# Four small moves around the change from the embedding product to the gate stage in a hybrid encoder layer: where two frames live, when the lower gate rows load, when the second pair is transposed, and which queue loads h

## The chip, the cores and the metric

The kernel runs on one core of a Trainium2 chip. The metric is device time in microseconds (us) of one execution, as the median of several executions; lower is better. A profile of one further execution is read beside it. TensorE is called PE in the profile, VectorE DVE, ScalarE ACT, GpSimd POOL and SyncE SP.

## What is computed

One layer of a streaming encoder over 2048 prompt rows and 32 decode rows, model width D = 1024, all in float32. Cut to what matters here (`N` is an RMS norm over a row, `rows` are the 2080 rows):

```python
z  = N(h, g_mix) @ w_in                       # six parts of 512 columns
y  = concat(conv_mixer(z), pooling_mixer(z))  # rows x 1024
h  = h + y @ w_out                            # the output projection
e  = p @ w_ple                                # the embedding product, p is rows x 256
h  = h + e * sigmoid(N(h, g_ple) @ w_gate)    # the gate
out = N(h, g_final)
```

The kernel also returns the new convolution and pooling states, which play no part here.

## The kernel before

**Number format.** Products of float32 values are made from halves: each operand is split into a high part (a cast on ACT) and the rest (a subtraction on DVE), and three of the four partial products are formed (`FINE`). The split operands are called frames below when they hold activations, and weight parts when they hold weights.

**Tiles and pairs.** The rows are cut into 17 row tiles: 0 to 15 of 128 rows, and tile 16 with the 32 decode rows. The output projection and the gate go over pairs of row tiles (0 and 1, 2 and 3, and so on; a pair is called by its first tile). One pair is one call of `seven`, a Strassen-Winograd scheme: seven products instead of eight, in the order

```
x 11   y 12   x S2*T2   z S1*T1   z S4*22   x S3*T3   x 22*T4
```

(two or three of them change places for certain pairs). A product is 12 matmuls of 128x128 by 128x512. 11, 12 and 22 are quadrants of a pair's transposed rows, S1 to S4 sums of them, T1 to T4 sums of the weight's quadrants. The results lie in PSUM banks called `x_o`, `y_o`, `z_o` in the output projection, and `x_g`, `y_g`, `z_g` in the gate. `carry` takes an intermediate result out of a bank (`c_o` by DVE, `c_g` by ACT), `out` finishes a quadrant. The dictionary `between`, the last argument of `seven`, holds work that is written down between two products: `step(1)` stands after the first, `step(2)` after the second, `step(3)` after the third, `step(4)` after the fourth. That work prepares the next pair.

**Stages.** After the input projection and the mixers comes the output projection for pairs 0 to 14; the new `h` goes to a buffer in device memory, `h_d` (`done_h`). The embedding product runs in parts (`embed`, L149 on): seven tiles early, and tiles 7 to 14 and 16 in a last part between the output projection and the gate. Its results go to `e_d` in device memory. Each tile of it needs a frame `pps_i`, loaded by `load_pps` (L128) from `pp_d`; the loads are issued up to three tiles ahead. Then comes the gate for pairs 0 to 14; after pair 4 the short tile 16 is worked in (`short_gate`).

**The gate's input.** A pair's upper tile `hn_i` is loaded by rows (`load_rows`, L396), copied by ACT (`ho`, L1530) and transposed by PE in eight transposes into two banks (`pth`, L1532); that is `turned`. The pair's lower tile `hn_{i+1}` is loaded in four quarters by SP (`by_quarters`, L1541) and transposed by DVE's stream transpose in place (`turned_here`, L1547). `prep_g(i)` returns two pieces of work: `first` (loads and the stream transpose) and `second` (PE's transposes, sums on DVE at L1728, splits at L81 and L84), to be done after the second and the third product of the pair before. For pair 2 the loads are issued ahead of that (`ahead`). For pair 0 the two pieces stand behind two of the embedding tiles.

**The gate's weights.** `g_d` in device memory holds the scaled gate weight. Its upper four blocks of rows are `wg_t` (`tops`), its lower four `wg_b` (`bots`, L1386). They are split into the parts 11, T1, T2, T3, 21, 22 and T4 by casts on ACT (L203) and subtractions on DVE (L195, L210); the last subtraction, at L1776, makes T4's source, and after it the lower rows are read for the last time. The embedding weights (`wq`, L1504) lie in a slot that T2 and T4 use later.

**Buffers.** The pools that the change touches: `st` (four slots, tag `t`: carried results, and frames `pps`), `ss` (three slots, tag `s`: the frame sums of L1728 and those of the output projection), `xh` (four slots: `h`, and before it results of the embedding), `ya` (five slots: `hn`, `e`), `cmb` (eight slots: split frames, and `wg_b`). A load into a slot waits until the last reader of what was there before is done.

**What sets the order.** Every engine works in order through its own list, and so does each DMA queue's issuer: SP issues DMAs only, POOL issues DMAs between small computations, ACT some. The order of each list comes from a scheduler that weighs the instructions by its own estimates; the text of the program is one of its inputs, and two constructions tie it: `tc.issue_after(x)` puts what is inside behind `x`, and `keep_in_program_order` keeps single instructions where they are written. So a change of one place can reorder instructions at others. Loads of `h` for the gate are issued by POOL (0.53 us each), those of `hn` and `e` by SP. A finished tile goes out by POOL (L1578), and the last pair's output in four pieces (`normed`, L1643 and L1645).

Of the kernel before, what the change touches and what calls it, by code (L numbers as in the profile page):

```python
# [10 lines left out]
F32R = mybir.dt.float32r  # L11
# [4 lines left out]
P = 128  # L16
# [15 lines left out]
EARLY = 7  # L32
# [4 lines left out]
def trunk(ctx, tc, x_p, x_s, c_conv, c_pool, p_p, p_s, g_mix, w_in, conv_w, conv_b, pool_w,  # L37
          pool_scale, w_out, g_ple, w_gate, w_ple, g_fin, y_p, y_s, sc_p, sp_p, sc_s, sp_s):
    nc = tc.nc
# [6 lines left out]
    h_d = tc.dram_tile([T, D], F32, name="h_d")  # L46
# [33 lines left out]
    def split(hi, lo, src, eng=nc.vector, later=False):  # L80
        ins = nc.scalar.copy(hi, src)  # L81
        if later:
            tc.keep_in_program_order(ins)
        eng.tensor_tensor(lo, src, hi.bitcast(F32), op=ALU.subtract)  # L84
        return ins
# [15 lines left out]
    tiles = [(i * P, P) for i in range(SEQ // P)] + [(SEQ, DEC)]  # L101

    def rows_of(pr, sa, r, n):
        return pr[r:r + n] if r < SEQ else sa
# [22 lines left out]
    def load_pps(t, i, queue, ins=False):  # L127
        n = 4 * tiles[i][1]  # L128
        load = queue.dma_start(t.rearrange("p a k n -> p (a k n)")[:, :n].bitcast(F32), pp_d[i, :, :n])
        return load if ins else t  # L130
# [57 lines left out]
    def weight_source(W, q, k, top, bot, pin=False):  # L188

        b11, b12 = top[:, :NH], top[:, NH:]  # L190
        b21, b22 = (bot[:, :NH], bot[:, NH:]) if bot is not None else (None, None)
        t, x, y = {"11": (b11, None, None), "T1": (b11, b12, b11), "T2": (b11, b22, b11), "T3": (b12, b22, b12),
                   "22": (b22, None, None), "21": (b21, None, None), "T4": (b21, b21, b11)}[q]
        if x is not None:
            ins = nc.vector.tensor_tensor(t, x, y, op=ALU.subtract)  # L195
            if pin:
                tc.keep_in_program_order(ins)
        return t

    def weight_first(W, part, q, pin=False):  # L200

        k, t = part
        ins = nc.scalar.copy(W[q][0][:, k], t)  # L203
        if pin:
            tc.keep_in_program_order(ins)

    def weight_second(W, part, q, pin=False):

        k, t = part
        ins = nc.vector.tensor_tensor(W[q][1][:, k], t, W[q][0][:, k].bitcast(F32), op=ALU.subtract)  # L210
        if pin:
            tc.keep_in_program_order(ins)
        return ins

    def weight_parts(W, tops, bots, *names, order=range(KH), pin=False):

        for q in names:
            at = lambda k: (W, q, k, tops[k], bots[k] if bots else None)
            todo = [(k, weight_source(*at(k), pin)) for k in order[:2]]
            for k in order[2:]:  # L220
                weight_first(W, todo[0], q, pin)
                following = (k, weight_source(*at(k), pin))
                weight_second(W, todo.pop(0), q, pin)
                todo.append(following)
            for part in todo:
                weight_first(W, part, q, pin)
                ins = weight_second(W, part, q, pin)
        return ins
# [130 lines left out]
    def slot(name):  # L359
        return acts[0].tile([P, SLOT], F32R, tag="hn", name=name)  # L360
# [8 lines left out]
    def weight_slot(W, name, *names):  # L369
        t = slot(f"{name}_{names[0]}")  # L370
        c = halves(t)
        W.update({q: c[2 * i:2 * i + 2] for i, q in enumerate(names)})
        return t
# [8 lines left out]
    def ring4(t, name):  # L382
        return t.tile([P, D], F32, tag="t", name=name)
# [9 lines left out]
    def load_rows(pool, name, i, pr, sa=None, queue=nc.sync):  # L393
        r, n = tiles[i]
        t = ring4(pool, f"{name}_{i}")
        queue.dma_start(t[:n], pr[r:r + n] if sa is None else rows_of(pr, sa, r, n))  # L396
        return t

    with ExitStack() as s1:
# [414 lines left out]
        second = second_block()  # L814
# [382 lines left out]
        ahead = {}  # L1197
# [102 lines left out]
    with ExitStack() as s2:  # L1300
        pool = lambda name, bufs: s2.enter_context(tc.tile_pool(name=name, bufs=bufs, reuse_waits="tile"))
        qa, xh, ya, cmb = (pool(*a) for a in (("qa", 2), ("xh", 4), ("ya", 5), ("cmb", 8)))
# [122 lines left out]
        for c in range(EARLY):  # L1425
            if c == EARLY - 2:
# [3 lines left out]
        st, ss = (s2.enter_context(tc.tile_pool(name=name, bufs=bufs, side="right", reuse_waits="tile"))  # L1430
                  for name, bufs in (("st", 4), ("ss", 3)))
# [36 lines left out]
        for i in range(0, NT - 1, 2):  # L1468
# [6 lines left out]
            if last:  # L1475
                n = tiles[NT - 1][1]
# [19 lines left out]
        tops, _ = rows_of_weight(ya, "wg_t", g_d, 0)  # L1496
        weight_slot(W, "wg", *PLACES[0])
        weight_parts(W, tops, None, "11", "T1")
        shared = slot("wq")
        wp = [[shared[:, (2 * k + h) * D:(2 * k + h + 1) * D] for h in range(2)] for k in range(2)]  # L1500
        got = {0: load_pps(st.tile([P, 2, 2, P], F32R, tag="t", name=f"pps_{EARLY}"), EARLY, nc.sync)}
        for k in range(2):
            for h in range(2):
                nc.sync.dma_start(wp[k][h].bitcast(F32), wl_d[k][h])  # L1504
        got[1] = st.tile([P, 2, 2, P], F32R, tag="t", name=f"pps_{EARLY + 1}")
        second_pps = load_pps(got[1], EARLY + 1, nc.sync, True)
        with tc.issue_after(second_pps.ins):
            bots = rows_of_weight(cmb, "wg_b", g_d, 1)[0]
# [13 lines left out]
        def turned(i, t=None):  # L1522
# [9 lines left out]
                    nc.tensor.transpose(pt[:, k * P:k * P + n], o[:n, k], ident[:n, :n])  # L1532
                out.append(pt.rearrange("p (k t) -> p k t", k=KH))
            return out

        def by_quarters(i):

            r, n = tiles[i]
            t = ring4(ya, f"hn_{i}")
            for q in range(4):  # L1540
                nc.sync.dma_start(t[q * 32:q * 32 + 32].rearrange("p (g c) -> p g c", g=4),  # L1541
                                  h_d[r:r + P, q * 256:q * 256 + 256].rearrange("(g p) c -> p g c", p=32))
            return t

        def turned_here(t):

# [51 lines left out]
        def last_pair(i, A, before):  # L1598
# [7 lines left out]
            wp = []  # L1606
            chunk = lambda: wp.extend(load_wp(cmb, "wl", nc.sync))

            h = [load_rows(xh, "h", i + b, h_d, queue=nc.gpsimd) for b in range(2)]
            tt = nc.vector.tensor_tensor  # L1610
            carry, _ = gate_ops(h, [e], P, f"g{i}", i)
            hg = [ring4(ya, f"hg_{b}") for b in range(2)]
# [25 lines left out]
            def normed(b, rf):  # L1638
                r = tiles[i + b][0]
                o, y = hg[b], y_p[r:r + P]  # L1640
                cut = 5 * P
                fixed(nc.vector.tensor_scalar(o[:, :cut], o[:, :cut], scalar1=rf, scalar2=None, op0=ALU.mult))
                nc.sync.dma_start(y[:, :cut], o[:, :cut])  # L1643
                fixed(nc.scalar.activation(o[:, cut:], o[:, cut:], AF.Copy, scale=rf))  # L1644
                (nc.scalar if b else nc.gpsimd).dma_start(y[:, cut:], o[:, cut:])  # L1645

            cols_of = lambda half: slice(half * NH, half * NH + NH)
            at_last = {}
# [68 lines left out]
        def prep_g(i, ahead=False):  # L1717

            A, got = {}, {}
            whole = lambda t: t.rearrange("p k (g t) -> p k g t", g=4)  # L1720

            def put(q, src, view=lambda t: t):
                A[q] = cmb.tile([P, KH, 2, P], F32R, tag="c", name=f"g{i}_{q}")
                split(view(A[q][:, :, 0]), view(A[q][:, :, 1]), src)

            def comb(q, x, y, op, view=lambda t: t):
                t = ss.tile([P, KH, P], F32, tag="s", name=f"g{i}_f{q}")
                nc.vector.tensor_tensor(view(t), x, y, op=op)  # L1728
                return t

            lower = []

            def load():
                got["lower"] = by_quarters(i + 1)
                got["upper"] = load_rows(ya, "hn", i, h_d) if i else first_h

            if ahead:
                load()

            def first():  # L1740
                if not ahead:
                    load()
                lower.extend(turned_here(got["lower"]))

            def second():
                a21, a22 = lower
                s1 = comb("S1", a21, a22, ALU.add, whole)
                a11, a12 = turned(i, got["upper"])
                put("11", a11)
                s2 = comb("S2", s1, a11, ALU.subtract)  # L1750
                s3 = comb("S3", whole(a11), a21, ALU.subtract, whole)
                put("12", a12)
                put("S2", s2)
                s4 = comb("S4", a12, s2, ALU.subtract)
                put("S1", s1)
                put("S3", s3)
                put("S4", s4)
                put("22", a22, whole)

            S[i] = A  # L1760
            return {2: first, 3: second}

        S = {}
        steps = prep_g(0)
        for c in range(len(rest_e)):
            run(c)
            if c in (2, 4):
                steps[2 if c == 2 else 3]()
        W["T2"] = halves(shared)[2:]
        weight_parts(W, tops, bots, "T2")  # L1770
        W["T3"] = halves(seventh("wg_T3"))
# [22 lines left out]
        for i in range(0, NT - 3, 2):  # L1794
            A = S.pop(i)
            following = prep_g(i + 2, not i)
            h = [load_rows(xh, "h", i + b, h_d, queue=nc.gpsimd) for b in range(2)]
            e = [load_rows(ya, "e", i + b, e_d) for b in range(2)]
            seven(f"g{i}", A, W, *gate_ops(h, e, P, f"g{i}", i), following)
            done_g(i, h[0])  # L1800
            if i in (0, 2, 4):
                next(short_steps)
            if i + 2 < NT - 3:
                done_g(i + 1, h[1])
# [29 lines left out]
```

## Time and profile before

| | us |
|---|---|
| median of three executions | 932.08 (931.37 to 932.5) |
| the profiled execution's own time | 929.11 |
| its span, first to last instruction | 927.3 |
| PE busy | 902.0 |
| DVE busy | 697.1 |
| ACT busy | 458.5 |
| POOL busy | 158.9 |

The profiled execution is one execution beside the three. Its granted TensorE clock was 0.994 on the mean. In the views that follow, a row of a timeline gives the start, the duration, the engine, the line in the kernel, the operation, the tiles it writes and reads, the number of instructions put together in the row, and in brackets how long the engine had waited before it and for what. A row of the waits gives who waited for whom, the sum in us, how often, and the longest. Instructions with the same tile names but other numbers (`hn_0`, `hn_8`) have one name, `hn`.

### The profile page before, as it was taken

To read this page: it belongs to the slowest core of one execution; us is meant where nothing else is said; L and a number is where in the kernel's file an instruction comes from. 1 tells how busy PE (TensorE), PEld (TensorE's weight loads), DVE (VectorE), ACT (ScalarE), POOL (GpSimd) and SP (SyncE) were. 2 spreads that over 40 slices of the span, in tenths; PEclk is the share of its full clock that TensorE was granted. 3 is DMA by queue.
4 is the path that set the end of the run, shared out by engine and by line. 5 is a ranking of instruction groups with operands and counts; after the bars stand their busy time and mean duration, and the time that the engine had idled before them with its cause. 6 is when DMAs were issued, how large, how long until landed. Compare 5 with 4: busy or idle time off the path is not lost. (4 is left out here: it accounts for less than half of the span.)

```text
span 927.3 us, 12203 instructions
## 1 busy us (share of the span) xinstructions
PE 902.0 (97%) x4186; PEld 723.5 (78%) x4186; DVE 697.1 (75%) x1148; ACT 458.5 (49%) x828; POOL 158.9 (17%) x309
## 2 busy tenths in 40 slices
PE   8999999999999999999999998999999999999995
PEld 6788888878888788766688886878888778778885
DVE  6895789797993687746668679765655988888884
ACT  7752555465453354523344376434434965555553
POOL 2200121122121122100010021111111311121212
PEclk9999999999999999999999999999999999999998
DMA  8164396747599675777743695867768876476652
GB/s 277 47 206 169 104 270 188 227 153 235 174 339 428 165 226 177 246 219 236 235 145 131 225 320 166 264 224 238 223 220 276 306 249 193 165 227 206 218 186 105
DMA packets 113243, 199.56 MB, mean 215 GB/s; under 512 B 13206, under 2 KB 69950, under 8 KB 112157
## 3 DMA queue, kind: packets, MB, share of 16 engines
q1 hardware_dynamic: 88733, 117.19, 40.4%
q0 software_dynamic: 22000, 77.21, 24.6%
q10 hardware_dynamic: 2448, 4.39, 1.3%
q8 instruction: 33, 0.54, 0.2%
q14 instruction: 29, 0.24, 0.1%
HBM read 133.06 MB, written 65.67 MB: 214 GB/s over the span
## 5 line engine op out<-in xcount | busy, mean ns | idle before, releaser
L185 PE MATMUL x_o<-wo,y 128*128 128x512 f32 x192 | 47.1, 400 | 3.4 <-DVE x L1315 3.4
L185 PE MATMUL z_g<-wg,g_S 128*128 128x512 f32 x192 | 47.4, 393 | 0.7 <-ACT c_g L1558 0.7
L185 PE MATMUL z_o<-wo,y_S 128*128 128x512 f32 x192 | 47.4, 389 | 0.0
L185 PEld LDWEIGHTS x_o<-wo,y 128*128 128x128 f32 x192 | 37.1, 194 | 11.8 <-issue 3.8
L185 PE MATMUL x_o<-wo_T,y_S 128*128 128x512 f32 x192 | 46.2, 390 | 0.0
L185 PEld LDWEIGHTS z_g<-wg,g_S 128*128 128x128 f32 x192 | 35.5, 188 | 8.5 <-ACT c_g L1558 1.3
L646 PE MATMUL z_ch<-B,w_ch_S 128*128 128x512 f32 x168 | 40.8, 392 | 1.2 <-ACT U L966 1.2
L185 PEld LDWEIGHTS z_o<-wo,y_S 128*128 128x128 f32 x192 | 36.0, 188 | 7.5
L185 PEld LDWEIGHTS x_o<-wo_T,y_S 128*128 128x128 f32 x192 | 35.9, 188 | 7.6 <-DVE c_o L1315 0.2
L646 PE MATMUL x_ch<-B,w_ch_S 128*128 128x512 f32 x168 | 41.8, 392 | 0.0
L646 PE MATMUL x_zab<-B,w_zab_S 128*128 128x512 f32 x168 | 40.9, 392 | 0.2 <-DVE w_zab_S L84 0.2
L646 PE MATMUL z_zab<-B,w_zab_S 128*128 128x512 f32 x168 | 41.1, 392 | 0.0
L646 PE MATMUL x_zbv<-B,w_zbv_S 128*128 128x512 f32 x168 | 40.8, 391 | 0.0
L646 PE MATMUL z_zbv<-B,w_zbv_S 128*128 128x512 f32 x168 | 40.7, 391 | 0.0
L646 PEld LDWEIGHTS z_ch<-B,w_ch_S 128*128 128x128 f32 x168 | 31.3, 188 | 8.9 <-ACT U L966 1.6
L646 PEld LDWEIGHTS x_zab<-B,w_zab_S 128*128 128x128 f32 x168 | 31.3, 188 | 7.9 <-issue 0.8
L646 PEld LDWEIGHTS x_zbv<-B,w_zbv_S 128*128 128x128 f32 x168 | 31.3, 188 | 7.7 <-issue 0.8
L646 PEld LDWEIGHTS z_zab<-B,w_zab_S 128*128 128x128 f32 x168 | 31.2, 188 | 7.5 <-issue 0.8
L646 PEld LDWEIGHTS x_ch<-B,w_ch_S 128*128 128x128 f32 x168 | 31.3, 188 | 7.3 <-issue 0.8
L646 PEld LDWEIGHTS z_zbv<-B,w_zbv_S 128*128 128x128 f32 x168 | 31.3, 188 | 7.2 <-issue 0.8
L1577 DVE SCALAR_TENSOR_TENSOR h<-h,rstd_f,g_bc 128x1024 f32<-128x1024 f32 (+1 forms) x15 | 19.3, 1284 | 14.6 <-POOL rstd_f L77 13.0
L94 ACT ACTIVATE junk<-x 128x1024 bf16<-128x1024 f32 (+1 forms) x17 | 18.0, 1056 | 22.6 <-DVE x L1315 21.1
(561 smaller groups left out, 2297.9 us busy)
## 6 DMA issues: line engine op xcount, KB each, us to landing
wn<-in_w_in_dram SPq DMA_DIRECT2D x24, 512.0 KB, 3.8
p_dT<-T POOLq DMA_DIRECT2D x16, 512.0 KB, 5.2
y<-y_d SPq DMA_DIRECT2D x16, 512.0 KB, 5.9
h<-h_d POOLq DMA_DIRECT2D x16, 512.0 KB, 5.1
e<-e_d SPq DMA_DIRECT2D x15, 512.0 KB, 4.7
x<-in_x_prompt_dram SPq DMA_DIRECT2D x14, 512.0 KB, 4.0
out_dram<-h POOLq DMA_DIRECT2D x14, 512.0 KB, 3.4
B<-p_d POOLq DMA_DIRECT2D x3, 2048.0 KB, 15.7
```

The costliest lines, as they stand in the source:

```text
L94: ins = nc.scalar.activation(junk[:n], x[:n], AF.Square, accum_out=ssq[:n])
L185: nc.tensor.matmul(ps[:n], lhs[:, k, a, :n], w[b][:, k], start=start and k + q == 0, stop=k == KH - 1 and q == 2, skip_group_check=True)
L646: nc.tensor.matmul(ps, lhs[:, k, x], b[:, k, y], start=start and k + q == 0, stop=stop and k == KH - 1 and q == 2, skip_group_check=True)
L1577: nc.vector.scalar_tensor_tensor(h[:n], h[:n], rf[:n], g_bc[:n], op0=ALU.mult, op1=ALU.mult)
```

## The change

1. `by_quarters` is defined earlier, and the quarter loads of `hn_1`, pair 0's lower tile, are written ahead of the loads of the frames. `prep_g(0)` takes that tile as given.
2. The first two frames of the last embedding part, `pps_7` and `pps_8`, take slots of `ss` instead of `st`. The lower gate rows stay behind the load of `pps_8` by `issue_after`, and so behind another slot than before.
3. For pair 2 (`ahead`) the second piece of `prep_g` is put after the fourth product instead of the third. For pair 0 nothing changes there: `steps[c // 2 + 1]` is the same as before.
4. The loads of `h` for pairs 6 to 12 and for the last pair are issued by SP instead of POOL, and so is one piece of the last pair's output (384 columns of its first tile).

```diff
         weight_parts(W, tops, None, "11", "T1")
+        def by_quarters(i):
+
+            r, n = tiles[i]
+            t = ring4(ya, f"hn_{i}")
+            for q in range(4):
+                nc.sync.dma_start(t[q * 32:q * 32 + 32].rearrange("p (g c) -> p g c", g=4),
+                                  h_d[r:r + P, q * 256:q * 256 + 256].rearrange("(g p) c -> p g c", p=32))
+            return t
+
+        first_lower = by_quarters(1)
         shared = slot("wq")
...
-        got = {0: load_pps(st.tile([P, 2, 2, P], F32R, tag="t", name=f"pps_{EARLY}"), EARLY, nc.sync)}
+        got = {0: load_pps(ss.tile([P, 2, 2, P], F32R, tag="s", name=f"pps_{EARLY}"), EARLY, nc.sync)}
         for k in range(2):
             for h in range(2):
                 nc.sync.dma_start(wp[k][h].bitcast(F32), wl_d[k][h])
-        got[1] = st.tile([P, 2, 2, P], F32R, tag="t", name=f"pps_{EARLY + 1}")
+        got[1] = ss.tile([P, 2, 2, P], F32R, tag="s", name=f"pps_{EARLY + 1}")
         second_pps = load_pps(got[1], EARLY + 1, nc.sync, True)
         with tc.issue_after(second_pps.ins):
             bots = rows_of_weight(cmb, "wg_b", g_d, 1)[0]
...
-            h = [load_rows(xh, "h", i + b, h_d, queue=nc.gpsimd) for b in range(2)]
+            h = [load_rows(xh, "h", i + b, h_d) for b in range(2)]      # last_pair
...
-                (nc.scalar if b else nc.gpsimd).dma_start(y[:, cut:], o[:, cut:])
+                (nc.scalar if b else nc.sync).dma_start(y[:, cut:], o[:, cut:])
...
             def load():
-                got["lower"] = by_quarters(i + 1)
+                got["lower"] = by_quarters(i + 1) if i else first_lower
...
-            return {2: first, 3: second}
+            return {2: first, 4 if ahead else 3: second}
...
             if c in (2, 4):
-                steps[2 if c == 2 else 3]()
+                steps[c // 2 + 1]()
...
-            h = [load_rows(xh, "h", i + b, h_d, queue=nc.gpsimd) for b in range(2)]
+            h = [load_rows(xh, "h", i + b, h_d, queue=nc.gpsimd if i < 6 else nc.sync) for b in range(2)]
             e = [load_rows(ya, "e", i + b, e_d) for b in range(2)]
```

More of the change, by code (lines that the diff above doesn't have):

```diff
@@ L1534, in turned @@
             return out
[L1536 to L1543, printed above, removed]
         def turned_here(t):
```

## The prediction

> **What bounds the kernel now.** I read first the busy times of the page, then PE's waits, then PE's timeline around those waits that lie where the change acts, and last the timelines of the engines that those waits name.
>
> ```profile
> span 927.3 us, 12203 instructions
> PE 902.0 (97%) x4186; PEld 723.5 (78%) x4186; DVE 697.1 (75%) x1148; ACT 458.5 (49%) x828; POOL 158.9 (17%) x309
> ```
>
> PE works for 97% of the span. The change takes no matmul away, so it can only win idle time of PE, and 25 us of that exist, most of it at the start and behind the last matmul. What lies in between is in PE's waits (us in total, times, longest):
>
> ```profile
> PE x_o L185 <- DVE x L1315: 3.4, 1, 3.4
> ...
> PE pth L1532 <- ACT ho L1530: 1.8, 2, 1.2
> PE e L109 <- DMA pps<-pp_d: 1.6, 1, 1.6
> ...
> PE z_g L185 <- ACT c_g L1558: 0.7, 1, 0.7
> PE x_g L185 <- DVE c_g L1566: 0.6, 1, 0.6
> ```
>
> The first is early in the output projection, which the change leaves alone. The other four, 1.8 + 1.6 + 0.7 + 0.6, are in the last embedding part and the gate stage. PE's timeline (start, duration, tile, matmuls in the group, wait before it) places them:
>
> ```profile
> 705.36 2.88 PE L185 MATMUL x_o<-wo_T,y_S 128*128 128x512 f32 x12
> ...
> 716.24 5.61 PE L109 MATMUL e<-wq,pps 128*128 128x512 f32 x24
> 721.69 1.03 PE L1532 MATMUL pth<-ident,ho 128*128 128x128 f32 x8
> 724.30 16.60 PE L109 MATMUL e<-wq,pps 128*128 128x512 f32 x72 [1.57 <-DMA pps<-pp_d]
> 740.73 2.01 PE L137 MATMUL e<-wq,pps 128*64 128x512 f32 x8
> ...
> 745.32 2.88 PE L185 MATMUL y_g<-wg,g 128*128 128x512 f32 x12
> ...
> 752.15 1.18 PE L1532 MATMUL pth<-ident,ho 128*128 128x128 f32 x8 [1.22 <-ACT ho L1530]
> ...
> 759.52 3.01 PE L185 MATMUL z_g<-wg,g_S 128*128 128x512 f32 x12 [0.73 <-ACT c_g L1558]
> ...
> 767.82 2.88 PE L185 MATMUL y_g<-wg,g 128*128 128x512 f32 x12
> ...
> 816.44 2.88 PE L185 MATMUL y_g<-wg,g 128*128 128x512 f32 x12
> ...
> 822.59 1.18 PE L1532 MATMUL pth<-ident,ho 128*128 128x128 f32 x8 [0.54 <-ACT ho L1530]
> ...
> 832.79 3.02 PE L185 MATMUL x_g<-wq,g 128*128 128x512 f32 x12 [0.62 <-DVE c_g L1566]
> ...
> 838.14 2.88 PE L185 MATMUL y_g<-wg,g 128*128 128x512 f32 x12
> ...
> 878.16 2.88 PE L185 MATMUL y_g<-wg,g 128*128 128x512 f32 x12
> ...
> 898.10 2.88 PE L185 MATMUL y_g<-wg,g 128*128 128x512 f32 x12
> ```
>
> The last two rows are the yardstick. A gate pair that waits for nothing takes 898.10 − 878.16 = 19.94 us from one y_g to the next: seven products and eight transposes. A product is 12 matmuls; 24 of them take 721.69 − 716.24 = 5.45, so one product is 2.725 and the transposes are 19.94 − 7 × 2.725 = 0.87. Against that:
> - Change-over, 716.24 to 745.32, is 29.08 us. It holds eight embedding products (21.80), one set of transposes (0.87) and tile 16 with the first gate product (745.32 − 740.73 = 4.59): 27.26. Lost: **1.82**.
> - First gate pair, 745.32 to 767.82, is 22.50. Lost: 22.50 − 19.94 = **2.56** (the waits 1.22 and 0.73 and PE's restarts behind them).
> - The pair from 816.44 to 838.14 is 21.70. Lost: **1.76** (0.54, 0.62 and restarts).
>
> Together 6.14 us is all that there is to win near the change.
>
> **The change part by part.** *Frames and lower gate rows.* SP's issues (one in-order queue) before:
>
> ```profile
> 699.08 0.81 SPq L1541 DMA_DIRECT2D hn<-h_d  x2
> ...
> 713.14 0.32 SPq L129 DMA_DIRECT2D pps<-pp_d  x1
> 713.50 3.03 SPq L1386 DMA_DIRECT2D wg_b<-g_d x4
> 716.63 16.46 SPq L129 DMA_DIRECT2D pps<-pp_d  x7
> 741.42 1.81 SPq L1541 DMA_DIRECT2D hn<-h_d  x4
> 743.35 1.07 SPq L396 DMA_DIRECT2D hn<-h_d  x1
> ```
>
> pps_8 waits for a slot of the `st` ring until 713.14; the four lower gate rows stand behind it by their tie, and pps_9 behind them, at 716.63. PE wants pps_9 behind pair 0's transposes, at 721.69 + 0.87 = 722.56, and gets it 1.57 late. In the changed instruction order pps_7 and pps_8 take slots of the frame-sum ring whose last readers end in the pair before (about 692), and the lower rows issue as PE releases their four slots, from about 697 to 706. The weights and pps_9 follow; pps_9 has no slot to wait for, so it issues near 711, 5.6 before its old 716.63. That covers 1.57 three times, so I take 1.7 of the 1.82 as won. What is late next there would be pps_10, which still waits for an `st` slot; it is a product and a half later and I see no row that makes it late.
>
> The earlier lower rows pull the gate weights forward. DVE and ACT before:
>
> ```profile
> 719.04 1.24 DVE L1547 STREAM_TRANSPOSE hn<-hn 128x1024 f32<-128x1024 f32 x1
> ...
> 740.68 2.49 DVE L1776 TENSOR_TENSOR wg_b<-wg_b,wg_t 128x512 f32<-128x512 f32 x4
> ```
>
> ```profile
> 708.32 1.14 ACT L1530 COPY ho<-hn 128x512 f32<-128x512 f32 x2 [7.34 <-DMA hn<-h_d]
> ...
> 751.48 1.14 ACT L1530 COPY ho<-hn 128x512 f32<-128x512 f32 x2 [4.01 <-DMA hn<-h_d]
> ```
>
> DVE works on these weights without a gap up to L1776, whose subtraction frees the slots into which hn_3 and hn_2 are loaded (741.42 and 743.35 above). hn_2 lands late, ACT's copies for it start at 751.48, and PE's 1.22 follows. After the change ACT's casts of wg_11 stand ahead of ho_0 instead of behind it, so they no longer sit through the 7.34 us, and DVE's chain can start about 4 us earlier; I take 4, from 740.68 to about 737. Nothing is saved in DVE's work, it is only moved.
>
> *Second pair's transposes.* In pair 0's seven products they move from behind the third to behind the fourth, 2.73 us later. Wanted then at about 752.15 − 1.22 + 2.73 less the 1.7 won before = 752.0; hn_2, loaded 4 us earlier, has its copies ready at about 751.48 + 1.14 − 4 = 748.6. So the 1.22 goes with 3 us to spare, and the copy c_g (which stood on ACT behind these copies and the 1.07 of casts) comes ahead of them: the 0.73 goes too. What could be late next is the second pair's own frames, whose casts and sums now start a product later; three matmuls of the next pair stand ahead of this pair's last product in the new order as a filler. I keep 0.2 for it: 2.56 − 0.2 = 2.36 won. The two edits overlap: with the earlier load alone most of the 1.22 would go anyway.
>
> *The quarter load of hn_1* moves up in the text only; it waits for the same slot (its first quarter went at 699.08), so its transfers cost nothing new. But DVE's stream transpose of it (1.24) now stands ahead of the carry of the last output-projection pair, on an in-order engine. The row of the landing is
>
> ```profile
> hn<-h_d SPq DMA_DIRECT2D x9, 128.0 KB, 3.5
> ```
>
> so the last of four quarters, issued about 1.4 behind the first (699.08), lands near 704.0, the transpose ends at 705.2 and the carry (some 0.6) at 705.8. PE needs it for the x_o that began at 705.36; in the new order three matmuls of y_o (0.68) stand ahead of that, so at 706.04. Zero at this landing, 1.0 at the 4.7 of SP's larger loads (row below); I allow up to 2. I take 0.1.
>
> *h loads and the last output piece by SP.* Ten loads and one store leave POOL. The issues cost POOL 0.53 each and SP some 0.34; neither is on the path. What counts is the wait of the first such load:
>
> ```profile
> POOL h L396 <- DMA out_dram<-h: 20.0, 10, 3.7
> ```
>
> ```profile
> 815.21 0.61 POOL L1578 DMA_DIRECT2D out_dram<-h  x1 [1.62 <-DVE h L1577]
> 819.48 0.53 POOL L396 DMA_DIRECT2D h<-h_d  x1 [3.66 <-DMA out_dram<-h]
> ```
>
> An h load needs the slot from which an output tile is being stored. On POOL that wait blocked little; on SP it blocks what stands behind it. In the new order of SP, h_7 waits for the store of tile 4, and hn_8 stands right behind it. (In later pairs the hn loads stand ahead of the h load that waits.) Shifted by the 4.1 won so far the store issues at 811.1, h_7 at 815.4, hn_8 at 815.7. Loads of that size on SP land as
>
> ```profile
> e<-e_d SPq DMA_DIRECT2D x15, 512.0 KB, 4.7
> ```
>
> so hn_8 is there at 820.4 and its first copy (0.57) at 821.0. PE's transposes of it, which in the new order follow seven matmuls later (7/12 × 2.725 = 1.6), are wanted at 816.44 − 4.1 + 2 × 2.725 + 1.6 = 819.4. Lost: 1.6 at that landing, nothing if the store completes a microsecond and a half earlier (its DVE work moves in the new order too). I take 0.8. Against it the old 0.54 and 0.62 and their restarts, 1.76, go: the first because of those seven matmuls, the second because the sums behind it start earlier relative to their product; I take all but 0.1.
>
> The Trainium skill, "DMA: Bandwidth & Descriptors", section on queues, rings and completion order, says that a DMA engine alternates between the queue rows that have work, a packet at a time. By that rule hn_8 loses by standing in one row behind h_7's half megabyte, where before POOL's row took it beside SP's. The row for the rate is this (0.84 of the DMA engines busy at 315 GB/s, so 375 when full):
>
> ```profile
> 716.00:745.00 29.00, 27.43 (x125) 22.04 (x124) 28.63 (x47) 23.96 (x47) 8.80 (x16) 1.00 0.84 315
> ```
>
> Half a megabyte takes 0.524 / 0.375 = 1.4 us there. As a mechanism of this kernel that is a further 1.4 us for hn_8, and it enters the first rival.
>
> *Tail.* The last store to be issued is ACT's, and POOL's piece is early:
>
> ```profile
> 916.29 0.65 POOL L1645 DMA_DIRECT2D out_dram<-hg  x1 [0.95 <-ACT hg L1644]
> ...
> 920.93 0.38 ACTq L1645 DMA_DIRECT2D out_dram<-hg  x1
> ```
>
> On SP it may issue at most some 4 us later than on POOL and still be no later than ACT's: zero, within 0.2 either way.
>
> *Sum:* −1.7 − 2.36 + 0.1 − 1.66 + 0.8 = −4.8; with the rounding of the restarts I say −4.8 ± 1.4.
>
> **The rivals.**
> - *Late hn_8* (0.18). Everything up to the first gate pair is won, but hn_8 is late by the full 1.6 + 1.4 = 3.0: −1.7 − 2.36 + 0.1 − 1.66 + 3.0 = −2.6, that is 929.5. For it: one queue, two half megabytes. Against: the store has to be as late as the shift alone makes it.
> - *The waits only move* (0.12). The stream transpose ahead of the carry costs its 2 us, ACT or DVE are late with the second pair's frames by as much as PE gained, and the pps wait goes to pps_10: about zero, 932. For it: DVE was busy without a gap from 710 to 750, so PE arrives earlier at an engine that has no slack. Against: that chain starts earlier itself.
> - *SP stuck behind h_7* (0.07; slower). If the store of tile 4 holds SP until hn_8 costs PE more than the 5.6 won elsewhere (4.8 + 0.8), the kernel is slower; with 2 us beyond, 934. For that h_7 would have to issue at 819.4 − 0.6 − 4.7 − 0.3 + 7.6 = 821.4, 10 us after its store where the row above shows 4.3. The longest such wait was 3.7 us, hence the small chance.
>
> **How the numbers follow.** The profiled execution took 929.11 us, 1.8 over its span and 2.97 under the median of the runs, 932.08. The sum makes it 924.3; on the median's side 932.08 − 4.8 = 927.3. A measurement can tell about 0.2%, 1.9 us. The forecast has 0.63; its own range is 925.9 to 928.7. The late hn_8 ends below 930.2 and so counts as faster too, the moved waits as same, SP stuck as slower: faster 0.81, same 0.12, slower 0.07. The range takes in all 6.14 won with 0.7 for the measurement (925.2) and reaches up to most of the second rival (931.5).
>
> **What would show it.** In the new trace: no wait of e for pps, and pps_9's issue near 711; L1776 near 737 and hn_2's copies on ACT without a wait of several microseconds; the transposes of pair 2 behind z_g without a wait, and y_g to y_g in the first pair near 20.1 instead of 22.50. The pair that had 21.70 shows pth waiting for ho by 0 to 1.6 and nothing else. It would be wrong if x_o or z_o waited for DVE's carry near 706, if the frames of the second pair came late (a wait of x_g for g), or if SP stood still before an L396 load of h for more than 6 us.

## The result and the profile after

The changed kernel takes 928.75 us (median of 8, 926.38 to 930.89) against 932.52 for the kernel before (8, 931.37 to 933.27). The ratio is 0.9967 (95% interval 0.9953 to 0.9981): faster by 3.1 us with the ratio, 3.8 with the medians. 927.3 was predicted, within 925.2 to 931.5.

Among these sixteen, the executions of the changed kernel lie wider apart (4.5 us) than those of the kernel before (1.9); timed more often beside the experiments below, the kernel before spreads as wide (6.1 to 7.6 us in 17 to 29 executions). The one that was profiled took 926.38, the shortest of the eight, with a span of 924.4; the profiled execution of the kernel before, at 929.11, was also shorter than every one of its eight.

PE's waits in the changed kernel, from the profile (sum, times, longest, in us):

```profile
PE x_o L185 <- DVE x L1315: 3.4, 1, 3.4
PE x_o L185 <- DVE c_o L1315: 2.6, 1, 2.6
...
PE x_g L185 <- DVE c_g L1567: 0.3, 1, 0.3
```

The waits for pps, for ho and for ACT's c_g are gone. A new one of 2.6 us stands in their place, in the last pair of the output projection. PE's timeline after, where the lines of the prediction were:

```profile
700.86 1.52 PE L185 MATMUL z_o<-wo,y_S 128*128 128x512 f32 x6
...
706.30 0.84 PE L185 MATMUL y_o<-wo,y 128*128 128x512 f32 x3
709.76 3.04 PE L185 MATMUL x_o<-wo_T,y_S 128*128 128x512 f32 x12 [2.62 <-DVE c_o L1315]
...
720.11 13.77 PE L109 MATMUL e<-wq,pps 128*128 128x512 f32 x60
...
747.35 2.88 PE L185 MATMUL y_g<-wg,g 128*128 128x512 f32 x12
...
755.52 1.03 PE L1542 MATMUL pth<-ident,ho 128*128 128x128 f32 x8
...
767.31 2.88 PE L185 MATMUL y_g<-wg,g 128*128 128x512 f32 x12
...
815.79 2.88 PE L185 MATMUL y_g<-wg,g 128*128 128x512 f32 x12
...
822.82 1.03 PE L1542 MATMUL pth<-ident,ho 128*128 128x128 f32 x8
...
831.04 3.06 PE L185 MATMUL x_g<-wq,g 128*128 128x512 f32 x12 [0.34 <-DVE c_g L1567]
...
836.43 2.88 PE L185 MATMUL y_g<-wg,g 128*128 128x512 f32 x12
```

The same half product z_o is in the timeline of the kernel before as

```profile
699.92 1.52 PE L185 MATMUL z_o<-wo,y_S 128*128 128x512 f32 x6
```

It is the mark from which stretches are counted, because profiles differ ahead of the change already (this z_o starts anywhere from 699.92 to 703.54 in the profiles of this case). The last matmuls, first before and then after, are

```profile
916.86 0.88 PE L109 MATMUL e_l<-wl,pps_l 128*128 128x256 f32 x6
```

```profile
915.11 0.88 PE L109 MATMUL e_l<-wl,pps_l 128*128 128x256 f32 x6
```

The differences of starts, with the end of the last matmul and the end of the span:

| stretch, us | before | after | difference |
|---|---|---|---|
| mark to first e | 16.32 | 19.25 | +2.93 |
| first e to first y_g (change-over) | 29.08 | 27.24 | −1.84 |
| first to second y_g (first gate pair) | 22.50 | 19.96 | −2.54 |
| to the y_g at 816 | 48.62 | 48.48 | −0.14 |
| the pair that had 21.70 | 21.70 | 20.64 | −1.06 |
| three further pairs | 59.96 | 59.96 | 0 |
| last y_g to the last matmul's end | 19.64 | 19.60 | −0.04 |
| last matmul's end to the span's end | 9.56 | 8.41 | −1.15 |
| from the mark on | 227.38 | 223.54 | −3.84 |

Two lines are far from the prediction's sum: +2.93 ahead of the embedding, where it had +0.1, and −1.15 behind the last matmul, where it had 0. DVE's timeline after shows the first:

```profile
701.06 0.69 DVE L1315 TENSOR_TENSOR c_o<-x_o,x 128x512 f32<-128x512 f32 x1
707.88 1.25 DVE L1548 STREAM_TRANSPOSE hn<-hn 128x1024 f32<-128x1024 f32 x1 [6.13 <-DMA hn<-h_d]
709.05 0.65 DVE L1315 TENSOR_TENSOR c_o<-x_o,x 128x512 f32<-128x512 f32 x1
```

DVE stands for 6.13 us before the stream transpose of hn_1; the carry c_o, whose matmuls had ended at 705.1, is behind it, and x_o on PE waits for the carry. In the kernel before, the same carry ran as soon as its product was done, ahead of the stream transpose (719.04):

```profile
704.20 0.69 DVE L1315 TENSOR_TENSOR c_o<-x_o,x 128x512 f32<-128x512 f32 x1 [3.39 <-PE x_o L185]
```

SP's timeline after (start, time of issue, number):

```profile
700.49 2.32 SPq L1504 DMA_DIRECT2D hn<-h_d  x4
702.91 3.90 SPq L1386 DMA_DIRECT2D wg_b<-g_d  x4
706.92 0.37 SPq L396 DMA_DIRECT2D hn<-h_d  x1
712.83 1.74 SPq L1514 DMA_DIRECT2D wq<-wl_d  x4
714.61 19.62 SPq L129 DMA_DIRECT2D pps<-pp_d  x7
739.53 2.10 SPq L1504 DMA_DIRECT2D hn<-h_d  x4
```

The quarters were issued from 700.49 to 702.81, and the last to land did so at 707.88, 5 us after its issue; two megabytes of lower rows go out right behind them. The DMA engines are full from 704 to 710 (the last two columns are the busy share of the 16 DMA engines and GB/s; the third from the right is PE's granted clock):

```profile
704.00:708.00 4.00, 3.14 (x14) 2.25 (x12) 0.12 (x1) 1.50 (x3) 0.00 (x0) 1.00 0.98 314
708.00:710.00 2.00, 0.24 (x1) 0.24 (x2) 2.00 (x3) 0.68 (x2) 0.00 (x0) 1.00 1.01 410
```

The later parts went as the diff reads: the subtraction at L1777 begins at 738.78 instead of 740.68, and ACT's copies of hn_2 wait 0.70 instead of 4.01:

```profile
749.36 1.14 ACT L1540 COPY ho<-hn 128x512 f32<-128x512 f32 x2 [0.70 <-DMA hn<-h_d]
```

### The profile page after: what moved, and what is told of

It reads as the page before. It is cut to its first block, busy times and chain, and to the rows that moved or that the text cites. A ratio compares the mean times of both kernels' runs of the same rounds, so it can differ in the third digit from the quotient of the medians.

```text
span 924.4 us, 12206 instructions
## 1 busy us (share of the span) xinstructions
PE 901.5 (98%) x4186; PEld 723.4 (78%) x4186; DVE 696.1 (75%) x1148; ACT 458.4 (50%) x828; POOL 155.9 (17%) x298
## 3 DMA queue, kind: packets, MB, share of 16 engines
q10 hardware_dynamic: 2448, 4.39, 1.3%
```

## The experiments

Unless told otherwise, an experiment is the changed kernel with one edit. Ratios are to the kernel before on the same chip, with 95% intervals; the changed kernel's is 0.9967 (0.9953 to 0.9981), and 0.001 is 0.93 us. Two theories were weighed: (A) the late transfer of hn_1 blocks the carry on DVE, and that wait is a real loss; (B) the waits only move, since something else is late there.

**The stream transpose of hn_1 behind the carries.**

```diff
-                lower.extend(turned_here(got["lower"]))
+                with tc.issue_after(summed[-4].ins) if not i else ExitStack():
+                    lower.extend(turned_here(got["lower"]))
```

> The changed kernel, with one tie added: DVE's stream transpose of hn_1 stands behind the last carries of the output projection (as in the kernel before) and not ahead of them. Theory A (in the changed kernel DVE, in order, sits 6.13 us before that transpose, the carry c_o behind it is late, and PE's x_o waits 2.62 plus a restart): this wait disappears, 928.75 - 2.9 = 925.9. Theory B (the wait only moves: the transpose and the weight work behind it come later, and PE waits for gate frames or for pps instead): 928 to 929.5.

926.81 us (6 executions, 924.14 to 927.54), ratio 0.9938 (0.9924 to 0.9952). The same kernel once more, on another chip:

> The same kernel as the first of these runs (the changed kernel with the stream transpose of hn_1 tied behind the last carries, nothing else), timed beside the one before and, by the ratio to the kernel before, to the changed kernel. If the tie is worth its 2.6: a ratio of 0.993 to 0.994 again, against 0.9967 of the changed kernel.

925.71 (6, 924.92 to 926.33), ratio 0.9926 (0.9909 to 0.9944). Both lie under the changed kernel, by 2.7 and 3.8 us. The wait for c_o is gone and the stretch from the mark to e is 16.55 and 16.32 again. A new and smaller wait stands behind, in the first of the two:

```profile
718.54 1.48 PE L109 MATMUL e<-wq,pps 128*128 128x512 f32 x4
720.79 13.00 PE L109 MATMUL e<-wq,pps 128*128 128x512 f32 x56 [0.77 <-DMA wq<-wl_d]
```

The change-over is 28.73 there (29.14 in the second), 27.24 in the changed kernel: PE comes 1.6 earlier and wq is not there yet. So A is right that the wait is a loss, and B that part of it moves: 1.5 and 1.9 of the 2.93 come back in the change-over. From the mark to the end these two profiles gain only 1.2 and 0.6 us (222.3 and 223.0 against 223.54), less than the medians. The profiled execution of the changed kernel is its shortest and lacks a fall of PE's clock (below) that most profiles with this wait have; that would fit the rest, but was not shown.

**Without the early quarter loads** (part 1 undone):

```diff
-        first_lower = by_quarters(1)
...
-                got["lower"] = by_quarters(i + 1) if i else first_lower
+                got["lower"] = by_quarters(i + 1)
```

> The changed kernel without its first part: the quarter loads of hn_1 are written where they were before. Theory A: the stream transpose stands late on DVE again, the 2.62 us wait of x_o is gone and the rest of the gain stays: about 926. Theory B (the early quarter loads are what lets the lower rows and the weights start early): the waits of before in the first gate pair come back, 930 to 932.

928.74 (12, 927.07 to 932.60), ratio 0.9962 (0.9950 to 0.9974): no difference to the changed kernel. The wait for c_o is gone as A says, but the profile (of the longest execution, 932.60) has e waiting for wq twice, 1.89 and 0.78, and a change-over of 32.47. The quarters, the lower rows and wq were issued between 703.88 and 715.5 there, wq landed 10.8 us after its issue, and the granted clock stood at 0.50 for 3.4 us behind the waits. That one transfer gains what another loses is argued from this, not shown. The theory's 926 was missed.

**pps_7 and pps_8 in the `st` ring** (part 2 undone):

```diff
-        got = {0: load_pps(ss.tile([P, 2, 2, P], F32R, tag="s", ...
+        got = {0: load_pps(st.tile([P, 2, 2, P], F32R, tag="t", ...
```

(and the same for pps_8)

> The changed kernel with pps_7 and pps_8 in the st ring as before (parts 1, 3 and 4 stay). If the ring of the frames carries the gain at the change-over: pps_9 is late by about 1.6 again and hn_2 and hn_3 load some 3 us later, beside the 2.62 of the carry: 928.75 + 1.8 to + 3.5, that is 930.5 to 932.3. If the ring is idle: 928.75.

934.03 (12, 931.76 to 936.49), ratio 1.0017 (1.0001 to 1.0034): about 4.7 us worse than the changed kernel, more than forecast, and slower than the kernel before. pps_8 is issued at 716.08, the lower rows at 716.81, pps_9 only at 719.85, and PE loses 7 us in the change-over (34.41): 3.71 in one wait behind pair 0's transposes, where pps_9 is due, and some 3 more (half of the 5.6 us of work from 732.3 on) because the granted clock stands at 0.50 from 731.1 to 737.9. Without the ring the other parts gain nothing here.

This run also shows that the lower rows are not needed to make hn_1 late. They no longer stand right behind the quarters, and the stream transpose still begins 5 us after the last quarter's issue; x_o waits 2.20:

```profile
702.05 2.26 SPq L1504 DMA_DIRECT2D hn<-h_d  x4
...
716.81 2.94 SPq L1386 DMA_DIRECT2D wg_b<-g_d  x4
```

```profile
709.31 1.25 DVE L1548 STREAM_TRANSPOSE hn<-hn 128x1024 f32<-128x1024 f32 x1 [5.72 <-DMA hn<-h_d]
```

**The second pair's transposes behind the third product** (part 3 undone):

```diff
-            return {2: first, 4 if ahead else 3: second}
+            return {2: first, 3: second}
```

> The changed kernel with the second pair's transposes behind the third product, as before. In the changed kernel's trace ACT's copies of hn_2 start at 749.36 and end at 750.50, and the third product ends at about 752.8. If the earlier load alone removes the wait: 928.75, with no wait of pth for ho. If the later place is needed (casts and copies queue on ACT): waits of 0.7 to 2 in the first gate pair, 929.5 to 930.8.

930.54 (12, 928.87 to 933.33), ratio 0.9980 (0.9970 to 0.9991): 1.2 us above the changed kernel, though the two intervals overlap. The profile has the loss in two places. In the first gate pair it is only 0.60 (20.56 instead of 19.96), with a wait of 0.33 for c_g and none for ho. The rest is three pairs further on, where nothing was edited: 21.69 instead of 20.64, the 21.70 of the kernel before. So the forecast time was met, but more than half of the loss lies in a pair that the forecast did not name. In that pair the transposes stand seven matmuls into the third product, as in the changed kernel (in the next run, where POOL issues these h loads, four stand behind two matmuls and four behind four), but hn_8 is late:

```profile
822.26 0.43 SPq L396 DMA_DIRECT2D hn<-h_d  x1
```

```profile
827.01 1.14 ACT L1540 COPY ho<-hn 128x512 f32<-128x512 f32 x2 [0.68 <-DMA hn<-h_d]
```

```profile
827.68 1.18 PE L1542 MATMUL pth<-ident,ho 128*128 128x128 f32 x8 [0.40 <-ACT ho L1540]
```

The scheduler's order ahead of it differs: POOL's store of tile 4, for which SP's h_7 and behind it hn_8 wait, is issued 1.27 us ahead of the pair's y_g, 2.09 in the changed kernel. This is the prediction's late hn_8. Whether the longer wait for c_g in that pair (0.72, 0.34 in the changed kernel) comes from it too is not shown.

**h loads and the last piece by POOL** (part 4 undone):

```diff
-            h = [load_rows(xh, "h", i + b, h_d, queue=nc.gpsimd if i < 6 else nc.sync) for b in range(2)]
+            h = [load_rows(xh, "h", i + b, h_d, queue=nc.gpsimd) for b in range(2)]
```

(and likewise the last pair's loads and its piece of 384 columns)

> The changed kernel without its fourth part: h loads and the last 384 columns' piece by POOL again. From the two traces: from the end of the last matmul to the end of the span it is 9.56 us before and 8.41 after; no h load on SP cost PE anything. Theory (the part is worth about 1.2, at the tail, and nothing in the pairs): 928.75 + 1.2 = 929.9, with 9.5 behind the last matmul and pairs as in the changed kernel. Rival (the tail only varies from run to run): 928.75. Rival (h loads by SP do cost the pairs something): 927 to 928.

930.07 (11, 928.89 to 932.13), ratio 0.9980 (0.9968 to 0.9992): 1.2 us above the changed kernel, again with overlapping intervals. In the profile the pairs are the same (20.62 for the one with hn_8); the time behind the last matmul is 9.57 again. So there the part is worth 1.15, all of it at the end. Three kernels ask which of its edits does that. Only the piece on POOL, first:

```diff
-                (nc.scalar if b else nc.sync).dma_start(y[:, cut:], o[:, cut:])
+                (nc.scalar if b else nc.gpsimd).dma_start(y[:, cut:], o[:, cut:])
```

> The changed kernel with only the last 384 columns' piece of the output's first tile back on POOL. If that piece alone sets the end of the span: 928.75 + 1.2 = 929.9 and 9.5 us behind the last matmul. If the h loads of the last pair do, or if the tail only varies: 928.75 and 8.4.

928.56 (5, 926.97 to 929.54), ratio 0.9958 (0.9944 to 0.9971): not worse, and 8.41 behind the last matmul. Then only the last pair's two h loads on POOL (`queue=nc.gpsimd` in `last_pair`), and only the eight of pairs 6 to 12 (`queue=nc.gpsimd` in the loop), one execution each:

> The changed kernel with only the last pair's two h loads on POOL again. It tells where the 1.15 us at the end come from: behind the last matmul 9.5 us if the last pair's loads set it, 8.4 if not.

> The changed kernel with only the h loads of pairs 6 to 12 on POOL again. Behind the last matmul 9.5 us if their number sets it, 8.4 if the last pair's loads do; between these if each of the ten DMAs of POOL's queue costs a tenth of it. The pairs themselves as in the changed kernel, 20.6 for the one with the late hn_8.

They took 927.34 and 928.05. In the second the pair with hn_8 takes 20.97, 0.4 more than expected. The end follows the number of h loads that POOL issues, wherever they stand:

| of the ten h loads on POOL | 0 | 2 | 8 | 10 |
|---|---|---|---|---|
| last matmul's end to the span's end, us | 8.41 | 8.59 | 9.36 | 9.57 |

About 0.115 us each, although the last of the eight is issued at 864.84, 52 us ahead of the last matmul's end. The ends of the table are well repeated (8.35 to 8.42 in the nine profiles of this case with none on POOL, 9.56 and 9.57 in the three with all ten); 2 and 8 have one profile each. What the time is spent on, the profile doesn't name.

**Part 2 alone, on the kernel before.** The same two lines of rings, nothing else.

> The kernel before with the second part alone: pps_7 and pps_8 in the ring of frame sums. If the ring carries the gain at the change-over and at the first pair: 932.5 - 1.8 to - 4.4, so 928 to 930.7, and no wait of x_o for c_o since the quarter loads are not first. If the lower rows, loaded ahead of the embedding weights, delay these (queues share the transfer rate): a wait of e for wq of 1 to 3, and 930 to 932.

929.41 (12, 928.30 to 932.21), ratio 0.9978 (0.9968 to 0.9987): faster by 2 us. The first gate pair is as good as in the changed kernel (19.93), so the lower rows' earlier load alone removes that loss. The change-over loses 2 us more than before (31.16): e waits for wq, 0.54 and 1.20, and more behind it (below).

**Less ahead of wq, and nothing ahead of it.** On the kernel with the transpose behind the carries, first the third and fourth lower row behind wq, then all four and hn_0:

```diff
-            bots = rows_of_weight(cmb, "wg_b", g_d, 1)[0]
+            bots = rows_of_weight(cmb, "wg_b", g_d, 1, range(2))[0]
+        with tc.issue_after(last_wq.ins):
+            bots += rows_of_weight(cmb, "wg_b", g_d, 1, range(2, KH))[0]
```

> The changed kernel with the stream transpose of hn_1 tied behind the last carries (as in the first of these runs, where e waited 0.77 for wq and lost 1.3 with the restart), and with the third and fourth of the lower gate rows loaded behind wq. Theory (wq is late because one megabyte more of lower rows is in flight ahead of it): wq lands 2 us or more sooner, no wait of e for wq, 926.81 - 1.3 = 925.5. Rival (the rows that come later delay the weight work on DVE): the wait goes to the first gate pair, 926.8 to 928.

925.08 (5, 924.53 to 926.18), ratio 0.9927 (0.9915 to 0.9939), the best median, but not to be told from the kernel without the split (0.9938 and 0.9926). And not by the mechanism expected: wq still lands 8.2 us after its issue (8.1 and 8.4 without the split), e still waits (0.24 and 0.77), and the first gate pair has 21.33.

```diff
-        with tc.issue_after(second_pps.ins):
+        with tc.issue_after(last_wq.ins):
             bots = rows_of_weight(cmb, "wg_b", g_d, 1)[0]
-        first_h = load_rows(xh, "hn", 0, h_d)
+        with tc.issue_after(last_wq.ins):
+            first_h = load_rows(xh, "hn", 0, h_d)
```

> The changed kernel with the stream transpose of hn_1 tied behind the last carries, and all four lower gate rows and hn_0 loaded behind the embedding weights wq. Theory (the DMA engines are full from 704 to 724 in every kernel here, so a transfer wins only what another one loses): wq lands after some 4 us and the wait of e for wq is gone (1.3), but the rows land 4 us later and the first gate pair waits for DVE's weight work; together within 1 us of the next kernel. Rival (the rows have slack): 1.3 us under the next kernel.

929.57 (12, 927.97 to 931.68), ratio 0.9973 (0.9960 to 0.9987): both expectations missed, 3 us and more worse than with the rows first. With no lower row ahead of it wq lands after 3.7 us and e no longer waits for it, and the first gate pair has 20.02, so the weight work is not late. But hn_0, now last in the queue, lands 14.9 us after its issue, and the scheduler had put its first transpose in the middle of the embedding (the clock stands at 0.50 for 3.4 us behind this wait):

```profile
730.16 0.33 PE L1543 MATMUL pth<-ident,ho 128*128 128x128 f32 x1 [3.07 <-ACT ho L1541]
```

The expectation's premise, DMA engines full from 704 to 724 in every kernel, doesn't hold here: from 708 to 712 they are 0.18 busy.

**A wait that costs more than its length.** The kernels with the wait for c_o all issue the same x_o behind it, but it doesn't take the same time. In the kernel with the piece on POOL:

```profile
710.24 5.49 PE L185 MATMUL x_o<-wo_T,y_S 128*128 128x512 f32 x12 [3.02 <-DVE c_o L1315]
```

```profile
708.00:710.00 2.00, 0.00 (x0) 0.00 (x0) 1.64 (x2) 0.75 (x2) 0.00 (x0) 0.85 0.99 381
710.00:712.00 2.00, 1.76 (x4) 1.48 (x5) 2.00 (x5) 0.00 (x0) 0.00 (x0) 0.50 1.03 420
712.00:714.00 2.00, 2.00 (x6) 1.51 (x6) 1.18 (x2) 0.00 (x0) 0.00 (x0) 0.50 0.67 272
714.00:716.00 2.00, 2.00 (x7) 1.51 (x6) 0.24 (x1) 0.00 (x0) 0.00 (x0) 0.50 0.00 0
```

The granted clock falls to 0.50 in the wait, at 709.4, and stays there for 6.8 us; the product takes 5.49 instead of 3.04. In the four other kernels with such a fall (last pair's, pairs' and all h on POOL, third product) it lasts 3.4 us. The stretch from the mark to e, where an undisturbed PE needs 16.32:

| kernel | wait for c_o | x_o behind it | mark to e |
|---|---|---|---|
| changed | 2.62 | 3.04 | 19.25 |
| frames in st | 2.20 | 3.02 | 18.82 |
| pairs' h on POOL | 2.01 | 4.61 | 20.26 |
| all h on POOL | 2.18 | 4.58 | 20.68 |
| last h on POOL | 2.88 | 4.39 | 20.90 |
| third product | 3.06 | 4.57 | 21.44 |
| last piece on POOL | 3.02 | 5.49 | 22.42 |

The profiled execution of the changed kernel is one of the two without this fall, and the shortest of its eight. The fall adds 1.4 to 2.8 us to a wait of 2 to 3 (mark to e, less 16.32, the wait and 0.3 for the restart). That it comes in some executions only can be part of the 4.5 us between the eight of the changed kernel: the mean clock on record is 0.996 for the four shortest and 0.992 to 0.994 for the four longest. It is not the whole reason, since the four at 0.996 still lie 2.3 us apart, and the kernel before, which has no such wait, spreads as wide. The same fall follows the waits for wq in the kernel with part 2 alone (0.58 from 720 to 722).

The Trainium skill, "TensorE: Matmul & The Clock Gate", part 1 on the clock gate, says that the clock falls to half after a window of about 3.4 us without work, that the window runs freely and so the moment varies, and that some 3.4 us of work bring it back. The half clock agrees, as do the 3.4 us that the fall lasted four times (6.8 the fifth) and the chance. The length of the wait does not: the shortest single wait after which it fell in the table was 2.01 us, under that window, and with part 2 alone it fell behind waits of 0.54 and 1.20 with one matmul between them.

## Why the prediction was right, and where it was not

*Right in sign and range, near in size*: −4.8 was forecast, −3.8 measured between the medians (−3.1 by the ratio) and −3.84 in the stretches of the two profiles. Term by term:

- *Change-over* (−1.7): measured −1.84. The wait for pps_9 is gone by the step given, a ring without a slot to wait for. pps_9 left at 714.61, not 711: SP was held by wq, since PE was 3 us late by then. The margin was smaller than argued, but enough.
- *First gate pair* (−2.36): measured −2.54. L1777 came 1.9 earlier and not 4, which with PE 2 us later at this place was still enough. That the earlier load would win most of it without part 3 was borne out: without part 3 the pair has 20.56, and with part 2 alone 19.93.
- *The quarter load of hn_1* (+0.1, with up to 2 allowed): **this step failed.** The mechanism was named, the size not. Measured: landing at 707.88 instead of 704.0, a wait of 2.62 and 2.93 with the restart, more with a fall of the clock. Two readings behind the 704.0 were wrong. The row at 699.08 holds two of the four quarters; in the kernel before the other two went at 703.01. And 3.5 us is the median of the nine quarter loads from 690 to 760, five of them in the gate behind 715, while hn_1's own took 5.5 (window 698 to 710):

```profile
699.08 0.81 SPq L1541 DMA_DIRECT2D hn<-h_d  x2
...
703.01 0.96 SPq L1541 DMA_DIRECT2D hn<-h_d  x2
```

```profile
hn<-h_d SPq DMA_DIRECT2D x4, 128.0 KB, 5.5
```

  The lower rows right behind the quarters are not needed for it, since with the frames in `st` they go 12 us later and the landing is as late; which of the other transfers there costs how much stays open. With the transpose behind the carries the wait is gone and the medians gain 2.7 to 3.8.
- *hn_8 behind h_7* (+0.8, rival up to +3.0): measured nothing in the changed kernel. The rows, POOL's store of tile 4 and then SP's h_7 and hn_8:

```profile
813.70 0.61 POOL L1579 DMA_DIRECT2D out_dram<-h  x1 [2.45 <-DVE h L1578]
```

```profile
816.93 0.34 SPq L396 DMA_DIRECT2D h<-h_d  x1
817.37 0.38 SPq L396 DMA_DIRECT2D hn<-h_d  x1
```

  h_7 went 3.2 us behind the store, not 4.3, and PE's transposes at 822.82 had no wait: PE was 3.4 us later than reckoned (818.51 for the product ahead of them instead of 819.16 − 4.1), for the most part through the wait for c_o that the prediction had put at nearly nothing. With all h loads on POOL the pair has the same 20.62. But the mechanism is real: without part 3 PE waits 0.40 for hn_8, and the pair loses 1.05, near the term's 0.8 and far from the rival's 3.0.
- *The pair that had 21.70* (−1.66): measured −1.06. The wait for ho went, the wait for c_g stayed with 0.34. No single part brings it: without part 3 the pair has 21.69 (with the late hn_8), without part 4 it has 20.62, and part 2 alone, with neither, already gives 20.84.
- *Tail* (0, within 0.2): measured −1.15, through the h loads and not through the piece.

The large errors partly cancel: +2.8 at hn_1 and +0.6 at the pair of 21.70 against −1.15 at the tail and −0.8 for hn_8. That the total came within 1 us is in part luck. The prediction's own sign of being wrong, x_o waiting for DVE's carry near 706, was seen. SP also stood 6.1 us before an h load of the last pair, at its mark of 6, and PE lost nothing by it (19.60 from the last y_g on, 19.64 before). The rival "the waits only move" came closest in kind: of 6.8 us won in the other stretches 2.93 went into the carry.

## What to carry to other kernels

A load that is moved to the front is a gain only for its own reader. What it stands ahead of, on the queue and on the in-order engine that reads it, pays: place the reader (here a transpose on DVE) behind the work that is already due, and take landing times of that very load, or of one in a stretch that is as full as the new one will be. Where the DMA engines are nearly full, as here from 704 to 724 (0.78 to 1.02 busy in each 4 us of the changed kernel), a reordering of loads can move a wait from one place to another; the end of a gap on PE is then worth checking for its clock, because a wait of 2 us can cost 4 (2.01 and 3.94 with the pairs' h on POOL).

## What was not expected of the hardware

Each 512 KB load of h that POOL issued instead of SP made the time behind the last matmul longer by about 0.115 us (8.41, 8.59, 9.36 and 9.57 for 0, 2, 8 and 10), even when the last of them was issued 52 us earlier. And the granted clock fell to 0.50 after waits of PE from 2.01 us on, in five of seven profiles with such a wait at the same place, not in the other two (2.20 and 2.62); two waits of 0.54 and 1.20 close together were followed by it as well.
